# Layer 1's conv, short-conv and gate projections as 512- plus 256-column products, four more modulation vectors by selector products, conv taps through ScalarE

## The chip, the cores and the metric

The kernel runs on one core of a Trainium2 chip. The metric is the device time of one launch in microseconds (us). Where the document speaks of TensorE, VectorE, ScalarE and GpSimd, the profile has PE (with PEld for the loading of weights), DVE, ACT and POOL; SP is the engine that issues most DMAs. 
## The reference

A two-layer trunk on 256 tokens of width 2048. In each layer a vector `c` gives six modulation vectors of 2048 (shift, scale and gate for the mixers, the same for the FFN); the normalised input is scaled and shifted by them, projected to 4288 columns, and these are split among four mixers.

```python
mod = (silu(c) @ w_mod[l] + b_mod[l]).reshape(bn, 6, d)      # 2048 x 12288
h = layer_norm(x) * (1.0 + scale_m) + shift_m
uv, q_c, kv_c, k_r, sb, sc, sh, ag = split(h @ w_in[l])      # 2048 x 4288
y_a = gmlp_mixer(uv)                                         # U, V below
y_b = mla_mixer(q_c, kv_c, k_r)                              # B: attention
y_c = sb * causal_dwconv(sc * sh, sconv_w, 3 taps)           # E * conv3(C)
y_d = silu(layer_norm(causal_dwconv(a * sigmoid(g), 31 taps)))   # D: ag = (a, g)
x = layer_norm(ALPHA * x + (1.0 + gate_m) * (concat(y_a, y_b, y_c, y_d) @ w_out[l]))
h = layer_norm(x) * (1.0 + scale_f) + shift_f
x = layer_norm(ALPHA * x + (1.0 + gate_f) * conv_ffn(h))     # up 2 x 5632, down 5632
```

## The kernel before

**Numbers.** Weights and activations are float32. To run at the rate of the faster matmul type, a weight tile is split in two parts, `whi` (a cast on ScalarE, line 455) and `wlo = w - whi` (a subtraction on VectorE, line 456), and the activations in the same way. A product is then the sum of three: high by high, high by low, low by high. Where activations are not ready in time the kernel multiplies in full float32 ("exact", tiles `wexact`), which needs no split and more time on TensorE.

**Two ways to write the three products.** `group` (line 478) makes, for each block of 128 channels and each of the 16 blocks of the contraction, three products of 256 columns (the tokens). `group2` (line 534), so far used by the FFN's up projection alone, lays the high and the low activations side by side, so that one product of 512 columns gives both terms with the high weights, and a product of 256 columns adds the low weights to the first half. One 512-channel group then fills four PSUM banks instead of two; the second half of each bank is added to the first when the bank is read (`second`, line 1416: a ScalarE copy of the second half, then a VectorE addition). There are six such banks (`accp`).

**Stages.** Layer 0's mixers go through `by_pieces` and are not touched. Layer 1's mixers (from line 1236 on) run the groups U, D, V, B, C, E in this order through `run` and `stream`: load and split one unit of 1 MB, issue the products of the unit before, then do a piece of the modulation stream (`pump`) and some pieces of background work. What a group's accumulators are for is done in `mix_u`, `mix_d`, `mix_v`, `mix_b`, `mix_c`, `mix_e`, at the start of the next group. D covers 1024 columns (a and g), C 1024 (`sc` and `sh`), E 512 (`sb`).

**Background.** The 31-tap convolution of D is a list of small pieces, of which `STEPS` says how many are done per unit. In layer 1 a piece is one tap of one channel block: a multiply-add on VectorE of 128 x 256 (`tap`, line 888); there are 124 of them. In layer 0 a piece is one tap of all four blocks: four ScalarE multiplications into a product tile (line 909, two such tiles in turn) and one VectorE addition of 128 x 1024 (line 910).

**Modulation vectors.** The matrix-vector product runs on VectorE: for each of 16 rows of blocks a multiply-add into an accumulator `macc` of 128 x 2048 (line 250). The sum over the 128 partitions is left to TensorE. `mod_cols` (line 198) multiplies each 128 x 128 block of the accumulator with a column of ones: one column out per product. `mod_rows` (line 220) splits the accumulator in high and low parts like a weight tile (`halves`, taking buffers of the same pool `splitp`, four each), multiplies them by selector columns that put the sum of each 512-column quarter in its own row of a 4 x 512 result, copies this, turns it with four small transposes and adds the bias. Which of the two is used is chosen in `settle`:

```python
elif (l, m) in ((1, SHIFT_F), (1, SCALE_F)):
    mod_rows(l, m, acc)
else:
    mod_cols(l, m, k0, acc[:, k0 * P : k1 * P])
```

So layer 1's FFN vectors go by rows; layer 0's FFN vectors (of which blocks 0 to 11 are summed in the output projection and 12 to 15 later) and layer 1's mixer vectors go by columns. These are needed by `to_hT` at the end of a layer half; its first instruction (`xn`) waits until the vectors are there.

**What sets the order.** The program text gives each instruction a rank. A planner goes through the program with its own estimates of durations and writes for each engine a fixed order: what is ready with the best rank goes next, so work of a later rank can be put ahead where the engine would stand. Tiles come from pools with a fixed number of buffers (11 `slot`, 10 `act`, 4 `tmp`, 4 `whi`, 4 `wlo`, 4 raw); an instruction that needs a new tile waits until one is free.

Of the kernel before, what the change touches and what calls it, by code (L numbers as in the profile page):

```python
# [13 lines left out]
P = 128  # L14
# [40 lines left out]
def encoder_kernel(ctx: ExitStack, tc: tile.TileContext, A: dict, consts: bass.AP, out: bass.AP):  # L55
# [155 lines left out]
            MOD[(l, m, k0 + j)] = cols[:, j : j + 1]  # L211
            MOD_BY[(l, m, k0 + j)] = done.ins.name

    def halves(acc, c0):
        hi = splitp.tile([P, 1024], F32R, tag="whi", name="mhi")
        lo = splitp.tile([P, 1024], F32R, tag="wlo", name="mlo")
        split((hi, lo), acc[:, c0 : c0 + 1024])
        return [(hi[:, i * 512 : (i + 1) * 512], lo[:, i * 512 : (i + 1) * 512]) for i in range(2)]

    def mod_rows(l, m, acc):  # L220

        ps = ms_tile("ps_row")
        for j, pair in enumerate(halves(acc, 0) + halves(acc, 1024)):
            for n, part in enumerate(pair):
                mm(ps[0:4, :], onesR[:, P + 4 * j : P + 4 * j + 4], part, j + n == 0, j + n == 4)
        row = tmp_tile("mrow")
        act.copy(row[0:4, :], ps[0:4, :])
        ps = ms_tile("ps_mod")
        for i in range(4):
            pe.transpose(ps[:, 4 * i : 4 * i + 4], row[0:4, i * P : (i + 1) * P], ident[0:4, 0:4])  # L230
        cols = keep.tile([P, KT], F32, name=f"mod_{l}_{m}")
        done = dve.scalar_tensor_tensor(
            out=cols.rearrange("p (i j) -> p i j", i=4),
            in0=ps[:, 0:KT].rearrange("p (i j) -> p i j", i=4),
            scalar=0.0 if m == SHIFT_F else 1.0,
            in1=bcol[l][:, m * KT : (m + 1) * KT].rearrange("p (j i) -> p i j", i=4),
            op0=ALU.add,
            op1=ALU.add,
        )
        for k in range(KT):  # L240
# [232 lines left out]
    def split(dst, src):  # L473
        hi, lo = dst[:2]
        act.copy(hi, src)  # L475
        dve.tensor_tensor(out=lo, in0=src, in1=hi.bitcast(F32), op=ALU.subtract)  # L476
# [384 lines left out]
    def mixers(l, w_in, Y, hF=None, between=None):  # L861
# [7 lines left out]
        CLB = lambda j: pm[:, 149 + j : 150 + j]  # L869


        def mix_d(cps, _):
            glu = slot("gluD").rearrange("p (j s) -> p j s", j=4)
            for b in range(2):
                sg = tmp_tile("sg")
                act.activation(out=sg, in_=cps[2 + b], func=AF.Sigmoid)
                dve.tensor_tensor(
                    out=glu[:, 2 * b : 2 * b + 2, :],
                    in0=cps[b].rearrange("p (j s) -> p j s", j=2),
                    in1=sg.rearrange("p (j s) -> p j s", j=2),  # L880
                    op=ALU.mult,
                )
            yd = slot("convD").rearrange("p (j s) -> p j s", j=4)
            def tap(j, k):
                if k == 30:
                    ident_act(yd[:, j, :], glu[:, j, :], CW(30, j), CB(j))
                else:
                    dve.scalar_tensor_tensor(
                        out=yd[:, j, 30 - k :],
                        in0=glu[:, j, : S - 30 + k],  # L890
                        scalar=CW(k, j),
                        in1=yd[:, j, 30 - k :],
                        op0=ALU.mult,
                        op1=ALU.add,
                    )

            prods = []

            def taps(k):
                n = S - 30 + k  # L900
                if k == 30:
                    for j in range(4):
                        tap(j, k)
                    return
                if len(prods) < 2:
                    prods.append(act_tile("prodD").rearrange("p (j s) -> p j s", j=4))
# [2 lines left out]
                    act.activation(out=pr[:, j, :n], in_=glu[:, j, :n], func=AF.Copy, scale=CW(k, j))  # L909
                dve.tensor_tensor(out=yd[:, :, 30 - k :], in0=yd[:, :, 30 - k :], in1=pr[:, :, :n], op=ALU.add)  # L910

            if l == 0:
                for k in range(30, -1, -1):
                    background.append(lambda k=k: taps(k))
            else:
                for j in range(4):
                    for k in range(30, -1, -1):
                        background.append(lambda j=j, k=k: tap(j, k))
            background.append(lambda: norm_d(yd))

        def norm_d(yd):
            Y["d"] = slot("yd").rearrange("p (j s) -> p j s", j=4)
# [273 lines left out]
                act.copy(Y["b"][:, 2 * b : 2 * b + 2, :], ps.rearrange("p (j s) -> p j s", j=2))  # L1196


        def mix_c(cps, _):
            ch = slot("chC").rearrange("p (j s) -> p j s", j=4)  # L1200
            for b in range(2):
                sc = tmp_tile("sc")
                act.copy(sc, cps[b])
                dve.tensor_tensor(
# [15 lines left out]
                        op1=ALU.add,  # L1220
                    )

        def mix_e(cps, _):
# [139 lines left out]
    def ffn_up(l, G):  # L1363
# [48 lines left out]

        for c0 in range(0, D_FF, 512):
            gi, j0 = c0 // 512, c0 // P

            def second(cps):

                out = []
                for b in range(2):
                    t = tmp_tile("second").rearrange("p (j s) -> p j s", j=2)  # L1420
                    for i in range(2):
                        act.copy(t[:, i, :], cps[2 * b + i][:, S:])
                        out.append(t[:, i, :])
                return out

            def gated(cps, j0=j0):
                G.append(slot("g").rearrange("p (j s) -> p j s", j=4))
# [191 lines left out]
```

## Time and profile before

| | |
|---|---|
| runs | 2282.78 us median of 3 (2282.72 to 2288.62) |
| profiled execution | 2281.42 us, of which the span of the trace is 2279.7 us |
| granted TensorE clock, mean | 0.991 |
| busy share of PE / DVE / ACT | 98% / 78% / 48% |
| layer 1's mixers after the D group | 1270 to 1435 us of the span |

The views that the prediction quotes: the page (busy shares, the chain of work that ended last); that chain in order of time; the busy time of each engine in chosen stretches, with the clock that TensorE was granted; the instructions of one tile, with count, shortest, median and longest duration in ns; the waits; and the timeline of one engine (start, length, what, and in brackets how long the engine had stood and for whom). A busy TensorE in these views is not TensorE at its peak: a product counts as busy while it waits for its turn in the pipeline, so the spacing of products says more than their durations.

### The profile page before, as it was taken

The numbers are of one execution on the slowest core, as the hardware profiler recorded it, in microseconds if no ns is written. First come the engines' busy times: TensorE is split into PE (matmuls) and PEld (weight loads), VectorE is DVE, ScalarE is ACT, GpSimd is POOL, SyncE is SP. The second block draws the span as 40 slices with busy tenths as digits, with TensorE's granted clock in tenths as the row PEclk, the third lists the DMA queues.
The fourth block names the chain that finished last, engine by engine and source line by source line (L and its number), as shares of the span: only waits on it lengthen the run. The fifth ranks groups of instructions, "written<-read, shape, count | busy, mean of one in ns | idle before, by whom it ended". The sixth has DMA issues, their size and how long they took to land.

```text
span 2279.7 us, 31503 instructions
## 1 busy us (share of the span) xinstructions
PE 2238.7 (98%) x12387; PEld 1934.8 (85%) x12387; DVE 1773.3 (78%) x2183; ACT 1098.2 (48%) x1644; POOL 35.1 (2%) x65
## 2 busy tenths in 40 slices
PE   7999999999999999999999999999999999999998
PEld 5788886798888888888789999889888888888886
DVE  5778988888888888988977899787676565565776
ACT  3356641354455444544454434545544454454553
POOL 0011000000000000000000000000000000000000
PEclk9999999999999999999999999999999999999999
DMA  9999699778888888898777677775666555555554
GB/s 349 385 373 359 256 328 349 249 278 314 311 307 315 314 312 327 303 346 302 273 236 254 201 242 250 271 273 177 240 240 215 192 185 197 191 185 194 187 191 148
DMA packets 228717, 605.21 MB, mean 265 GB/s; under 512 B 14660, under 2 KB 27188, under 8 KB 210900
## 3 DMA queue, kind: packets, MB, share of 16 engines
q1 hardware_dynamic: 227784, 602.30, 74.3%
q8 instruction: 97, 1.59, 0.3%
q0 software_dynamic: 784, 0.90, 0.1%
q14 instruction: 52, 0.43, 0.0%
HBM read 601.05 MB, written 2.10 MB: 265 GB/s over the span
## 4 chain that ended last, share of the span: by engine, by line
PE 88%; DVE 7%; DMA 2%; ACT 2%; issue 1%; POOL 0%; SPq 0%; DVEq 0%; ACTq 0%; POOLq 0%
PE g_c L83 22%; PE v_c L83 22%; PE d L83 20%; PE o L83 7%; PE D_c L83 3%; PE C_c L83 3%; PE B_c L83 2%; PE U_c L83 1%; PE E L83 1%; PE E_c L83 1%; DVE wlo L456 1%; PE ps_mod L83 1%; PE V L83 1%; DVE qacc L250 1%; DVE macc L250 1%
## 5 line engine op out<-in xcount | busy, mean ns | idle before, releaser
L455 ACT CAST whi<-wraw 128x1024 fp32r<-128x1024 f32 (+1 forms) x632 | 643.4, 1043 | 753.1 <-PE g_c L83 217.0
L456 DVE TENSOR_TENSOR wlo<-wraw,whi 128x1024 fp32r<-128x1024 f32 (+1 forms) x632 | 750.5, 1214 | 294.3 <-ACT whi L455 273.2
L83 PE MATMUL d<-whi,a 128*128 128x512 f32 x1344 | 390.3, 391 | 0.9 <-ACT whi L455 0.9
L250 DVE SCALAR_TENSOR_TENSOR macc<-wmod,cact,macc 128x2048 f32<-128x2048 f32 (+2 forms) x174 | 353.9, 2034 | 41.5 <-DMA wmod<-in_w_mod_dram 40.8
L83 PE MATMUL v_c<-hT,whi 128*128 128x512 f32 (+1 forms) x1456 | 343.1, 383 | 0.0
L83 PE MATMUL g_c<-hT,whi 128*128 128x512 f32 (+1 forms) x1344 | 313.5, 380 | 0.0
L83 PEld LDWEIGHTS v_c<-hT,whi 128*128 128x128 f32 x1456 | 264.6, 189 | 48.5
L83 PEld LDWEIGHTS d<-whi,a 128*128 128x128 f32 x1344 | 253.4, 189 | 54.5 <-ACT whi L455 2.2
L83 PEld LDWEIGHTS g_c<-hT,whi 128*128 128x128 f32 x1344 | 243.4, 189 | 43.5 <-DVE second L1436 0.4
L83 PE MATMUL d<-wlo,a 128*128 128x512 f32 x672 | 234.8, 392 | 1.6 <-DVE wlo L456 1.6
L83 PE MATMUL v_c<-hT,wlo 128*128 128x256 f32 x1400 | 190.7, 283 | 0.0
L83 PEld LDWEIGHTS v_c<-hT,wlo 128*128 128x128 f32 x1400 | 183.1, 191 | 6.6
L83 PE MATMUL g_c<-hT,wlo 128*128 128x256 f32 x1280 | 175.8, 283 | 0.0
L83 PEld LDWEIGHTS g_c<-hT,wlo 128*128 128x128 f32 x1280 | 168.2, 191 | 5.9
L83 PEld LDWEIGHTS d<-wlo,a 128*128 128x128 f32 x672 | 126.7, 189 | 30.1 <-DVE wlo L456 3.6
L475 ACT CAST a<-g 128x512 fp32r<-128x512 f32 x132 | 80.8, 619 | 91.1 <-PE d L83 89.4
L83 PE MATMUL o<-whi,a 128*128 128x512 f32 x384 | 111.3, 395 | 0.2 <-ACT whi L455 0.2
L476 DVE TENSOR_TENSOR a<-g,a 128x512 fp32r<-128x512 f32 x132 | 87.7, 684 | 9.2 <-ACT a L475 9.2
L250 DVE SCALAR_TENSOR_TENSOR qacc<-wmod,cact,qacc 128x1024 f32<-128x1024 f32 (+1 forms) x75 | 80.3, 1071 | 12.2 <-DMA wmod<-in_w_mod_dram 9.9
L83 PEld LDWEIGHTS o<-whi,a 128*128 128x128 f32 x384 | 72.7, 190 | 16.4 <-issue 0.7
L83 PE MATMUL D_c<-hT,whi 128*128 128x256 f32 x432 | 83.0, 292 | 2.4 <-ACT hT L475 1.6
L83 PEld LDWEIGHTS D_c<-hT,whi 128*128 128x128 f32 x432 | 69.5, 197 | 4.8 <-ACT hT L475 1.7
(370 smaller groups left out, 2619.1 us busy)
## 6 DMA issues: line engine op xcount, KB each, us to landing
wraw<-in_ffn_w_up_dram SPq DMA_DIRECT2D x168, 1024.0 KB, 5.0
wmod<-in_w_mod_dram SPq DMA_DIRECT2D x134, 1024.0 KB, 6.8
wraw<-in_ffn_w_down_dram SPq DMA_DIRECT2D x88, 1024.0 KB, 5.1
wraw<-in_w_in_dram SPq DMA_DIRECT2D x33, 1024.0 KB, 6.1
wmod<-in_w_mod_dram SPq DMA_DIRECT2D x64, 512.0 KB, 9.4
wraw<-in_w_out_dram SPq DMA_DIRECT2D x26, 1024.0 KB, 6.9
wmod<-in_w_mod_dram SPq DMA_DIRECT2D x32, 768.0 KB, 7.5
wexact<-in_w_in_dram SPq DMA_DIRECT2D x46, 512.0 KB, 7.9
```

The lines of the kernel that those rows point to most:

```text
L83: pe.matmul(o, lhsT, rhs, start=start, stop=stop, skip_group_check=True)
L250: i = dve.scalar_tensor_tensor(out=acc, in0=w, scalar=col, in1=acc, op0=ALU.mult, op1=ALU.add)
L455: act.copy(hi[:, :m], r)
L456: i = dve.tensor_tensor(out=lo[:, :m], in0=r, in1=hi[:, :m].bitcast(F32), op=ALU.subtract)
L475: act.copy(hi, src)
L476: dve.tensor_tensor(out=lo, in0=src, in1=hi.bitcast(F32), op=ALU.subtract)
```

## The change

- Layer 1's D, C and E go through `group2`. D becomes two groups of 512 channels, first the gate half g (`Dg`, folded and put through the sigmoid into a new tile `sgD` by `mix_dg`), then the half a; C becomes `Cs` (folded into a new tile `scC`) and C. `whole` folds four banks into a tile; `mix_d`, `mix_c` and `mix_e` then multiply in place.
- Layer 1's conv taps are done as in layer 0; `STEPS` counts the larger pieces.
- `mod_rows` takes 12 blocks as well as 16, and `settle` uses it for every vector whose first block is 0.
- `second` moves out of `ffn_up` unchanged.

```diff
 STEPS = [
     dict(B=3, C=2, up=2),
-    dict(U=5, V=5, B=4, C=6, E=6, up=2),
+    dict(U=1, V=1, B=1, C=2, E=2, up=2),
 ]
...
-    def halves(acc, c0):
+    def halves(acc, c0, width=1024):
...
-    def mod_rows(l, m, acc):
+    def mod_rows(l, m, acc, n=4):
 
         ps = ms_tile("ps_row")
-        for j, pair in enumerate(halves(acc, 0) + halves(acc, 1024)):
-            for n, part in enumerate(pair):
-                mm(ps[0:4, :], onesR[:, P + 4 * j : P + 4 * j + 4], part, j + n == 0, j + n == 4)
+        parts = [x for c0 in range(0, n * 512, 1024) for x in halves(acc, c0, min(1024, n * 512 - c0))]
+        for j, pair in enumerate(parts):
+            for i, part in enumerate(pair):
+                mm(ps[0:4, :], onesR[:, P + 4 * j : P + 4 * j + 4], part, j + i == 0, j + i == n)
...
-        elif (l, m) in ((1, SHIFT_F), (1, SCALE_F)):
-            mod_rows(l, m, acc)
+        elif k0 == 0:
+            mod_rows(l, m, acc, k1 // 4)
         else:
             mod_cols(l, m, k0, acc[:, k0 * P : k1 * P])
...
+    def second(cps):
+
+        out = []
+        for b in range(2):
+            t = tmp_tile("second").rearrange("p (j s) -> p j s", j=2)
+            for i in range(2):
+                act.copy(t[:, i, :], cps[2 * b + i][:, S:])
+                out.append(t[:, i, :])
+        return out
+
+    def whole(cps, dst):
+
+        for i, t in enumerate(second(cps)):
+            dve.tensor_tensor(out=dst[:, i, :], in0=cps[i][:, :S], in1=t, op=ALU.add)
...
-        def mix_d(cps, _):
+        def mix_d(cps, _=None):
             glu = slot("gluD").rearrange("p (j s) -> p j s", j=4)
-            for b in range(2):
+            if l > 0:
+                whole(cps, glu)
+                dve.tensor_tensor(out=glu, in0=glu, in1=Y["sg"], op=ALU.mult)
+            for b in range(2 if l == 0 else 0):
...
-            if l == 0:
-                for k in range(30, -1, -1):
-                    background.append(lambda k=k: taps(k))
-            else:
-                for j in range(4):
-                    for k in range(30, -1, -1):
-                        background.append(lambda j=j, k=k: tap(j, k))
+            for k in range(30, -1, -1):
+                background.append(lambda k=k: taps(k))
             background.append(lambda: norm_d(yd))
+
+        def mix_dg(cps):
+            Y["sg"] = slot("sgD").rearrange("p (j s) -> p j s", j=4)
+            whole(cps, Y["sg"])
+            act.activation(out=Y["sg"], in_=Y["sg"], func=AF.Sigmoid)
...
+        def mix_cs(cps):
+            Y["sc"] = slot("scC").rearrange("p (j s) -> p j s", j=4)
+            whole(cps, Y["sc"])
+
+        def mix_c(cps, _=None):
             ch = slot("chC").rearrange("p (j s) -> p j s", j=4)
-            for b in range(2):
+            if l > 0:
+                whole(cps, ch)
+                dve.tensor_tensor(out=ch, in0=ch, in1=Y["sc"], op=ALU.mult)
+            for b in range(2 if l == 0 else 0):
...
+        def mix_e(cps, _=None):
             yc = Y["c"]
+            if l > 0:
+                for i, t in enumerate(second(cps)):
+                    dve.tensor_tensor(out=t, in0=cps[i][:, :S], in1=t, op=ALU.add)
+                    dve.tensor_tensor(out=yc[:, i, :], in0=yc[:, i, :], in1=t, op=ALU.mult)
+                return
...
-        run(group(w_in, C_AG, 1024, f"D{l}", mix_d, spare=1))
+        run(group2(w_in, C_AG + 512, f"Dg{l}", mix_dg, spare=2))
+        run(group2(w_in, C_AG, f"D{l}", mix_d))
...
-        run(group(w_in, C_SC, 1024, f"C{l}", mix_c, bg=STEPS[l]["C"]))
+        run(group2(w_in, C_SC, f"Cs{l}", mix_cs, bg=STEPS[l]["C"]))
+        run(group2(w_in, C_SC + 512, f"C{l}", mix_c, bg=STEPS[l]["C"]))
         phase(l, "E")
-        run(group(w_in, C_SB, 512, f"E{l}", mix_e, nk=4, bg=STEPS[l]["E"]))
+        run(group2(w_in, C_SB, f"E{l}", mix_e, bg=STEPS[l]["E"]))
```

More of the change, by code (lines that the diff above doesn't have):

```diff
@@ L212, in mod_cols @@
             MOD_BY[(l, m, k0 + j)] = done.ins.name
-    def halves(acc, c0):
[L215 to L218, printed above, removed]
-    def mod_rows(l, m, acc):
+    def halves(acc, c0, width=1024):
+        hi = splitp.tile([P, 1024], F32R, tag="whi", name="mhi")[:, :width]
+        lo = splitp.tile([P, 1024], F32R, tag="wlo", name="mlo")[:, :width]
+        split((hi, lo), acc[:, c0 : c0 + width])
+        return [(hi[:, i : i + 512], lo[:, i : i + 512]) for i in range(0, width, 512)]
+    def mod_rows(l, m, acc, n=4):
         ps = ms_tile("ps_row")
-        for j, pair in enumerate(halves(acc, 0) + halves(acc, 1024)):
-            for n, part in enumerate(pair):
-                mm(ps[0:4, :], onesR[:, P + 4 * j : P + 4 * j + 4], part, j + n == 0, j + n == 4)
+        parts = [x for c0 in range(0, n * 512, 1024) for x in halves(acc, c0, min(1024, n * 512 - c0))]
+        for j, pair in enumerate(parts):
+            for i, part in enumerate(pair):
+                mm(ps[0:4, :], onesR[:, P + 4 * j : P + 4 * j + 4], part, j + i == 0, j + i == n)
         row = tmp_tile("mrow")
@@ L232, in mod_rows @@
         done = dve.scalar_tensor_tensor(
[L233 to L236, printed above, removed]
+            out=cols.rearrange("p (i j) -> p i j", i=4)[:, :, :n],
+            in0=ps[:, 0:KT].rearrange("p (i j) -> p i j", i=4)[:, :, :n],
+            scalar=0.0 if m in (SHIFT_M, SHIFT_F) else 1.0,
+            in1=bcol[l][:, m * KT : m * KT + 4 * n].rearrange("p (j i) -> p i j", i=4),
             op0=ALU.add,
@@ L239, in mod_rows @@
         )
-        for k in range(KT):
+        for k in range(4 * n):
             at = 4 * (k % 4) + k // 4
@@ L902, in taps @@
                     for j in range(4):
-                        tap(j, k)
+                        ident_act(yd[:, j, :], glu[:, j, :], CW(30, j), CB(j))
                     return
@@ L1221, in mix_c @@
                     )
-        def mix_e(cps, _):
+        def mix_e(cps, _=None):
             yc = Y["c"]
+            if l > 0:
[3 more added lines that the diff above has]
+                return
             for b in range(2):
@@ L1414, in ffn_up @@
             gi, j0 = c0 // 512, c0 // P
[L1416 to L1424, printed above, removed]
             def gated(cps, j0=j0):
```

13 lines of the change are left out of this document (removed).

## The prediction

> **What bounds the kernel now.** I read first the busy shares and the chain of waits on the page, then the same chain in order of time, then the busy time by stretch, and last the rows of the tiles that the change touches.
>
> ```profile
> span 2279.7 us, 31503 instructions
> PE 2238.7 (98%) x12387; PEld 1934.8 (85%) x12387; DVE 1773.3 (78%) x2183; ACT 1098.2 (48%) x1644; POOL 35.1 (2%) x65
> ...
> PE 88%; DVE 7%; DMA 2%; ACT 2%; issue 1%; POOL 0%; SPq 0%; DVEq 0%; ACTq 0%; POOLq 0%
> ```
>
> TensorE holds 88% of the chain that ended last. So time is saved where TensorE has less to do, and lost where another engine makes it wait. The stretch that the change rebuilds is layer 1 after its D group. Its four parts are shown by the first and the third of them and by the sum of the four (1270 to 1435 us); the columns are stretch, length, busy us of PE, PEld, DVE, ACT, POOL, granted clock, DMA share, GB/s:
>
> ```profile
> 1270.00:1305.00 35.00, 33.94 (x196) 29.62 (x194) 34.11 (x63) 18.64 (x25) 2.77 (x5) 1.00 0.50 157
> 1331.00:1406.00 75.00, 74.83 (x532) 69.68 (x533) 71.35 (x127) 29.26 (x48) 1.10 (x1) 1.00 0.70 246
> sum 165.00, PE 163.48 PEld 153.40 DVE 156.38 ACT 74.41 POOL 4.56; mean PE 40.87 PEld 38.35 DVE 39.10 ACT 18.60 POOL 1.14
> ```
>
> VectorE is as full there (156.4 of 165 us) as TensorE, and ScalarE is half empty (74.4). Yet VectorE seldom stops TensorE: the longest such wait listed there is this one.
>
> ```profile
> PE B_c L83 <- DVE wlo L456: 1.2, 1, 1.2
> ```
>
> So what is taken from VectorE there can bring about 1 us, not the tens that are taken off it.
>
> **The products.** From the chain in order of time (start, length, what, records):
>
> ```profile
> 1224.12 44.52 PE D_c L83 x371
> 1406.06 17.28 PE E_c L83 x144
> 1559.17 22.26 PE v_c L83 x128
> ```
>
> D and E go by three 256-column products: 17.28 / 144 = 0.120 us each, and 44.52 / 371 the same. A 512-channel group has 16 x 4 x 3 = 192 of them, 23.0 us. The FFN's group2, which D, C and E of layer 1 now use, does the same work in 64 + 64 products in 22.26 us. Saved: 0.77 us a group; D counts two groups, C two, E one, so **-3.9 us**.
>
> [...]
>
> **The modulation sums.** Four vectors move from mod_cols to mod_rows: SHIFT_F and SCALE_F of layer 0 (12 blocks) and SHIFT_M and SCALE_M of layer 1 (16). The late quarter (478 us) and the opening pieces keep mod_cols. The chain shows the old sums inside stages that TensorE bounds, and the new kind inside an FFN group of layer 0:
>
> ```profile
> 341.27 3.03 PE ps_mod L83 x28
> 393.89 2.57 PE ps_mod L83 x24
> 752.58 22.26 PE g_c L83 x128
> 777.02 1.62 PE v_c L83 x7
> 799.62 22.27 PE g_c L83 x128
> 1039.22 1.68 PE ps_mod L83 x16
> 1041.93 2.14 PE ps_mod L83 x20
> 1118.96 3.46 PE ps_mod L83 x32
> ```
>
> Old: 3.03 + 2.57 + (1.68 + 2.14) + 3.46 = 12.9 us. New: the v_c group from 774.84 to 799.62 holds one mod_rows of 16 blocks and lasts 24.78 instead of 22.27 us, so 2.5 us, its waits included. With 12 blocks two of its eight 512-column products fall away, each (22.26 - 64 x 0.120) / 64 = 0.23 us: 2.0 us. New sum 2 x 2.5 + 2 x 2.0 = 9.0. Saved: **-3.9 us**.
>
> **The clock behind the sums.** In these stretches the last-but-two column is the granted clock:
>
> ```profile
> 335.00:338.00 3.00, 3.00 (x15) 2.49 (x14) 2.77 (x2) 0.00 (x0) 0.00 (x0) 1.00 0.84 246
> 344.30:347.70 3.40, 3.40 (x10) 2.65 (x10) 3.36 (x2) 0.07 (x1) 0.00 (x0) 0.54 0.97 355
> 397.00:400.00 3.00, 3.00 (x9) 1.33 (x8) 1.05 (x4) 0.00 (x0) 0.00 (x0) 1.00 1.05 388
> 774.00:800.00 26.00, 26.00 (x151) 21.85 (x150) 24.28 (x29) 15.99 (x27) 0.00 (x0) 1.00 0.79 284
> 1043.00:1047.00 4.00, 4.00 (x18) 3.39 (x18) 1.98 (x2) 2.06 (x3) 0.00 (x0) 0.66 0.83 314
> 1122.40:1126.00 3.60, 3.60 (x11) 2.83 (x11) 2.30 (x2) 2.15 (x3) 0.00 (x0) 0.56 0.88 284
> ```
>
> Behind three of the four old sums the clock falls to about half for some 3.4 us; behind the one at 393.89, the shortest, it stays (row of 397). Around mod_rows at 774 it stays at 1.00. [...] Cost: 3.4 x (1 - 0.54) = 1.6, 4.0 x (1 - 0.66) = 1.4, 3.6 x (1 - 0.56) = 1.6. Removed: **-4.6 us**.
>
> [...]
>
> **Added work on the other engines.** In the tile views (count, then min/median/max ns):
>
> ```profile
> L888 DVE SCALAR_TENSOR_TENSOR convD<-gluD,pm,convD x120: 428/464/481, 1274.2 to 1399.2; 128x255 f32<-128x255 f32 x4, 128x254 f32<-128x254 f32 x4, 128x253 f32<-128x253 f32 x4, 128x252 f32<-128x252 f32 x4
> L909 ACT ACTIVATE prodD<-gluD,pm x120: 467/482/509, 190.4 to 276.2; 128x255 f32<-128x255 f32 x4, 128x253 f32<-128x253 f32 x4, 128x254 f32<-128x254 f32 x4, 128x252 f32<-128x252 f32 x4
> L910 DVE TENSOR_TENSOR convD<-convD,prodD x30: 1072/1156/1207, 193.5 to 280.3; 128x1020 f32<-128x1020 f32 x1, 128x1016 f32<-128x1016 f32 x1, 128x1012 f32<-128x1012 f32 x1, 128x1008 f32<-128x1008 f32 x1
>   DVE convD L910: 17.9, 11
> L1422 ACT COPY second<-v_c x84: 358/376/397, 526.7 to 2027.1; 128x256 f32<-128x256 f32 x84
> L1436 DVE TENSOR_TENSOR second<-v_c,second x84: 415/418/426, 527.1 to 2029.1; 128x256 f32<-128x256 f32 x84
> ```
>
> Taps: VectorE loses 120 x 0.464 = 55.7 and gains 30 x 1.156 = 34.7; ScalarE gains 120 x 0.482 = 57.8. Folding the second halves costs 4 copies and 4 additions a group: over Cs, C and E 12 x 0.376 = 4.5 on ScalarE and 12 x 0.418 = 5.0 on VectorE; the extra products in place are near what the old 512-wide ones cost. VectorE goes to about 156.4 - 55.7 + 34.7 + 5 = 140, ScalarE to 74.4 + 57.8 + 4.5 = 137, of a stretch that becomes about 160 us. Both hide behind TensorE as long as the weight casts, which share ScalarE's queue, stay on time: four split buffers hold two units ahead. In the C group a unit of 5.6 us asks ScalarE for two casts (2.1) and two taps (3.9), already 6.0; the attention block's products, which lie between, make room. From VectorE's relief I take the 1.2 us wait: **-1.0**. For hold-ups of casts behind taps, the lower end is nothing and the upper is layer 0's 17.9 us of ScalarE standing for convD (the fourth row); nearest to the lower end, since ScalarE keeps some 23 us free: **+2.0**.
>
> Banks: Dg to D, Cs to C, C to E and E to the output projection now pass four of six banks on; the lower end is nothing, the upper one folding of a bank pair (2 x 0.376 + 2 x 0.418 = 1.6 us) each, 6.4. The FFN passes them on the same way at 22.26 us a group, so **+0.5**. The two more tiles (sgD, scC) and the two product buffers fit the pools by my count of what is alive; nothing taken.
>
> Where the sums run: mod_rows needs split buffers and 2 x 1.2 us of VectorE per 16 blocks, mod_cols needed neither. For layer 1's two vectors VectorE has gaps of 4.38 and 1.40 us right behind the old sums, and ScalarE's casts wait there for DMA, so that buffers are free:
>
> ```profile
> L476 DVE TENSOR_TENSOR mlo<-macc,mhi x12: 1205/1220/1226, 260.2 to 2147.6; 128x1024 fp32r<-128x1024 f32 x12
> 1045.02 2.36 DVE L456 TENSOR_TENSOR wlo<-wraw,whi 128x1024 fp32r<-128x1024 f32 x2 [4.38 <-ACT whi L455]
> 1123.70 2.36 DVE L456 TENSOR_TENSOR wlo<-wraw,whi 128x1024 fp32r<-128x1024 f32 x2 [1.40 <-ACT whi L455]
> ACT whi L455 <- DMA wraw<-in_ffn_w_down_dram: 11.1, 7, 3.0
> ```
>
> Nothing to 2.4 us; taken 0. For layer 0's SCALE_F the accumulator ends late, while the next weights take the buffers:
>
> ```profile
> 390.33 1.81 DVE L250 SCALAR_TENSOR_TENSOR macc<-wmod,cact,macc 128x1536 f32<-128x1536 f32 x1
> 385.68 5.18 SPq L433 DMA_DIRECT2D wexact<-in_w_out_dram  x6
> 390.96 5.34 SPq L433 DMA_DIRECT2D wexact<-in_ffn_w_up_dram  x4
> 413.58 3.60 PE L83 MATMUL o<-wexact,yd 128*128 128x512 f32 x8
> 417.94 1.36 PE L594 MATMUL ps_xT<-cst,xn 128*128 128x128 f32 x8 [0.77 <-ACT xn L86]
> ```
>
> If the FFN's weights (third row) get the free buffers first, the second half of SCALE_F waits for the last products (until about 417) and needs some 3.3 us more, and xn, which waits for every modulation vector, and all FFN products stand behind it. Nothing to 3.3; **+1.0**.
>
> **Sum.** -3.9 - 3.9 - 4.6 - 1.0 + 2.0 + 0.5 + 1.0 = -9.9. Against the profiled execution's 2281.42 us this gives 2271.5; the median of the runs lies 1.4 above that execution, so I forecast **2273** for the median.
>
> **Rivals.** [...] *The vectors come late* at both layer ends: splits wait for buffers that the tail holds. Twice 3.3 instead of +1.0 once is +5.6: 2278.6. For it: xn is the first thing that TensorE waits for there (0.77). Against: the free buffers in layer 0's last stage, just shown. *ScalarE becomes the bound* in layer 1's B, C and E, the case of the other side: each of 30 taps holds the cast behind it as layer 0's eleven did (17.9 / 11 = 1.6 us), 49 us, of which the 23 us that ScalarE has free swallow their part; 26 us would land on TensorE instead of the 2.0 above: 2273 + 24 = 2297. It decides once casts come more than two units late. For it: 6.0 us asked per 5.6 us unit. Against: layer 0's waits came while VectorE was full. [...]
>
> **How the numbers follow.** Forecast as it stands, 2266 to 2276: 0.58. Clock 0.10, late vectors 0.10, ScalarE 0.14 (half of it over the bound below, half a milder 2280), merging or a shifted order of instructions 0.08. 0.3% is 6.8 us, about what a measurement of this kernel tells from no change: under 2275.9 is faster, over 2289.6 slower. Faster: 0.55 of the 0.58 and 0.05 from the mild ends of the others; slower: 0.07; the rest the same. The range runs from the full gain with no new cost (-13.4, 2269.4) less 4 for a lucky clock elsewhere, to the milder ScalarE case with both vectors late, 2286.
>
> **What would show it.** Right: no granted clock near 0.5 behind SHIFT_F, SHIFT_M and SCALE_M; D, C and E groups at 22.3 us; TensorE in 1270 to 1435 shorter by 3 to 4 us; ScalarE there near 137 us. Wrong: waits of TensorE for whi or wlo in layer 1's C, a gap over 1 us before the first transposes of xn, or ScalarE idle for convD before late casts.

## The result, and the profile after

The change makes the kernel slower: 2301.28 us median (2298.63 to 2309.67) against 2283.36 us (2282.72 to 2288.62) for the kernel before, a ratio of 1.0078 with a 95% interval of 1.0059 to 1.0097. The profiled execution took 2304.15 us, with a span of 2302.4 us, 22.7 us over that of before (2279.7). The forecast was 2273, its range ended at 2286: it was wrong, in sign too.

The page of the changed kernel, its span, busy shares and the shares of the chain that ended last:

```profile
span 2302.4 us, 30825 instructions
PE 2234.0 (97%) x11991; PEld 1909.8 (83%) x11991; DVE 1775.1 (77%) x2125; ACT 1156.0 (50%) x1789; POOL 37.7 (2%) x65
...
PE 85%; DVE 7%; DMA 4%; ACT 2%; issue 2%; POOL 0%; SPq 0%; DVEq 0%; ACTq 0%; POOLq 0%
```

TensorE is busy 4.7 us less than before, and the kernel lasts 22.7 us more. So the work went down as planned, and TensorE now waits where it did not wait. The chain in order of time (start, length, what, records) says in its gaps where; here the end of layer 0 and the first two groups of layer 1 that the change rebuilt:

```profile
1198.14 1.96 PE ps_row L83 x8
...
1212.08 1.97 PE ps_xT L610 x8
...
1247.40 22.29 PE Dg_c L83 x128
1269.69 22.27 PE D_c L83 x128
```

The two rebuilt groups last 22.3 us each, as forecast. But twelve microseconds lie between the last sum of a modulation vector (`ps_row`) and the first transposes of the normalised input (`ps_xT`). The timeline of TensorE shows the same at both ends of layer 0's second half, after the output projection `o` and after the down projection `d` (the brackets: idle before it, and for whom):

```profile
409.67 3.60 PE L83 MATMUL o<-wexact,yd 128*128 128x512 f32 x8
...
417.88 0.41 PE L231 MATMUL ps_mod<-cst,mrow 4*128 4x4 f32 x4 [0.66 <-ACT mrow L228]
428.79 1.97 PE L610 MATMUL ps_xT<-cst,xn 128*128 128x128 f32 x8 [10.50 <-ACT xn L86]
...
1194.78 0.39 PE L83 MATMUL d<-whi,a 128*128 128x512 f32 x1
...
1200.75 0.41 PE L231 MATMUL ps_mod<-cst,mrow 4*128 4x4 f32 x4 [0.66 <-ACT mrow L228]
1212.08 1.97 PE L610 MATMUL ps_xT<-cst,xn 128*128 128x128 f32 x8 [10.92 <-ACT xn L86]
```

Before, the wait for `xn` after `o` was 0.77 us (a row of the prediction). Now it is 10.50 and 10.92, and ahead of each the sums run in the open, after the stage's last product, for about 6 us. In each wait the clock falls to 0.50, and it stays there until 4.4 and 6.2 us after the products have begun again; the windows of TensorE (stretch, length, busy us of PE, PEld, DVE, ACT, POOL, granted clock, DMA share, GB/s):

```profile
419.50:433.20 13.70, 4.41 (x20) 4.22 (x21) 12.54 (x32) 8.07 (x19) 2.54 (x3) 0.50 0.36 130
1204.60:1218.30 13.70, 6.22 (x29) 6.04 (x30) 12.20 (x30) 8.77 (x20) 1.47 (x2) 0.50 0.17 63
```

**What is late, and why.** `xn` is made by ScalarE at the end of the normalisation of the first token tile, a chain of VectorE instructions that begins with `yg`. First the kernel before (timeline of VectorE), then the kernel after:

```profile
406.91 0.69 DVE L701 TENSOR_TENSOR yg<-o,gate 128x512 f32<-128x512 f32 x1 [8.79 <-PE o L83]
...
416.82 0.16 DVE L762 SCALAR_TENSOR_TENSOR rs_o0r<-m_o,rs_o0r 128x1 f32<-128x1 f32 x1 [0.67 <-POOL rs_o0r L114]
```

```profile
396.80 1.22 DVE L477 TENSOR_TENSOR mlo<-macc,mhi 128x1024 fp32r<-128x1024 f32 x1
409.92 0.69 DVE L477 TENSOR_TENSOR mlo<-macc,mhi 128x512 fp32r<-128x512 f32 x1 [11.90 <-issue]
413.36 1.99 DVE L477 TENSOR_TENSOR mlo<-macc,mhi 128x1024 fp32r<-128x1024 f32 x2 [2.74 <-PE o L83]
...
415.85 0.68 DVE L717 TENSOR_TENSOR yg<-o,gate 128x512 f32<-128x512 f32 x1
...
427.67 0.16 DVE L778 SCALAR_TENSOR_TENSOR rs_o0r<-m_o,rs_o0r 128x1 f32<-128x1 f32 x1 [0.67 <-POOL rs_o0r L114]
```

Before, `yg` started when the first token tile's products were done, 9.7 us ahead of the start of the last product (416.58, by the start times). The normalisation ran for some 10 us under the second token tile's products and cost TensorE nothing but its last microsecond. After, the four subtractions `mlo` (the last two in one row) that split the accumulators of layer 0's two FFN vectors stand ahead of `yg` in VectorE's fixed order, and the second and third of them wait 11.90 and 2.74 us. `yg` starts at 415.85, after the start of the last product (412.67), and the same normalisation now runs with TensorE standing by. The subtractions follow the casts `mhi` on ScalarE. Its timeline, at both ends, and VectorE's at the second:

```profile
408.15 0.62 ACT L476 CAST mhi<-macc 128x512 fp32r<-128x512 f32 x1 [16.12 <-PE o L83]
411.58 1.04 ACT L476 CAST mhi<-macc 128x1024 fp32r<-128x1024 f32 x1 [2.82 <-PE o L83]
...
1192.49 1.05 ACT L476 CAST mhi<-macc 128x1024 fp32r<-128x1024 f32 x1 [11.35 <-PE d L83]
```

```profile
1193.57 5.08 DVE L477 TENSOR_TENSOR mlo<-macc,mhi 128x1024 fp32r<-128x1024 f32 x4 [10.99 <-ACT mhi L476]
...
1198.65 0.68 DVE L717 TENSOR_TENSOR yg<-d,gate 128x512 f32<-128x512 f32 x1
```

A cast of an accumulator reads nothing that `o` or `d` makes. The profile infers that one of their products released it, and I read this as the wait for a buffer which that product was still using: the split buffers are held by the last chunk's weights until the last products. So the order is: products of the last chunk, split of the vectors, and only then the normalisation that before ran under these products.

### The profile page after: what moved, and what is told of

It reads as the page before. It is cut to its first block, busy times and chain, and to the rows that moved or that the text cites. A ratio compares the mean times of both kernels' runs of the same rounds, so it can differ in the third digit from the quotient of the medians.

```text
span 2302.4 us, 30825 instructions
## 1 busy us (share of the span) xinstructions
PE 2234.0 (97%) x11991; PEld 1909.8 (83%) x11991; DVE 1775.1 (77%) x2125; ACT 1156.0 (50%) x1789; POOL 37.7 (2%) x65
## 4 chain that ended last, share of the span: by engine, by line
PE 85%; DVE 7%; DMA 4%; ACT 2%; issue 2%; POOL 0%; SPq 0%; DVEq 0%; ACTq 0%; POOLq 0%
PE g_c L83 22%; PE v_c L83 21%; PE d L83 17%; PE o L83 6%; PE C_c L83 3%; PE D_c L83 2%; PE B_c L83 2%; DVE wlo L457 2%; PE U_c L83 1%; DVE qacc L251 1%; DVE macc L251 1%; DMA wmod<-in_w_mod_dram 1%; PE E L83 1%; DMA wraw<-in_ffn_w_down_dram 1%; PE Cs_c L83 1%
## 5 line engine op out<-in xcount | busy, mean ns | idle before, releaser
L915 ACT ACTIVATE prodD<-gluD,pm 128x255 f32<-128x255 f32 (+29 forms) x240 | 98.7, 486 | 29.9 <-DVE convD L916 29.7
L916 DVE TENSOR_TENSOR convD<-convD,prodD 128x1020 f32<-128x1020 f32 (+29 forms) x60 | 69.2, 1154 | 6.0 <-ACT prodD L915 5.4
```

## The experiments

The theory after the two traces: the loss sits wholly in the late vectors, because VectorE waits in the splits (11.90 and 2.74 us after `o`) with the normalisation behind them in its fixed order; the rest of the change is worth about what was forecast. The rivals: ScalarE or the taps hold up layer 1; the sums in rows cost more than they save wherever they stand; the half clock by itself is the loss.

This table gives the stages of the profiled execution of every kernel, worked out from the start times of products in TensorE's timeline (us). "o" and "d" run from the first to the last product of layer 0's projection, "wait" from there to the first transposes of `xn`, "up" from these to `d`, "U" from the transposes to layer 1's D, "D to E" from there to layer 1's output projection, "rest" to the end of the span.

| kernel | o | wait | up | d | wait | U | D to E | rest |
|---|---|---|---|---|---|---|---|---|
| before | 102.9 | 1.4 | 517.7 | 254.8 | 1.0 | 32.4 | 210.7 | 845.1 |
| after | 98.9 | 16.1 | 520.0 | 246.0 | 17.3 | 35.1 | 208.9 | 846.3 |
| e1 vectors early | 105.2 | 1.4 | 517.6 | 249.7 | 1.0 | 32.4 | 209.7 | 845.1 |
| e2 normalisation first | 99.8 | 6.9 | 518.6 | 245.5 | 8.5 | 34.0 | 212.4 | 846.6 |
| e3 no rows | 104.5 | 1.4 | 516.9 | 254.7 | 1.0 | 32.4 | 212.0 | 846.6 |
| e4 rows only | 97.9 | 16.1 | 517.7 | 245.4 | 17.3 | 34.0 | 209.9 | 844.8 |
| f1 products only | 102.9 | 1.4 | 517.1 | 254.9 | 1.0 | 32.4 | 206.9 | 847.5 |
| f2 taps only | 106.8 | 1.4 | 517.8 | 256.4 | 1.0 | 32.4 | 207.5 | 845.1 |
| f3 products, vectors early | 104.9 | 1.4 | 517.9 | 249.7 | 1.0 | 32.4 | 208.3 | 846.5 |
| f4 rows only, early | 104.4 | 1.4 | 518.8 | 249.7 | 1.0 | 32.4 | 211.1 | 846.5 |
| g1 early at `d` alone | 98.2 | 16.1 | 518.9 | 249.7 | 1.0 | 32.4 | 208.8 | 844.8 |
| g2 products, rows for layer 1 | 106.2 | 1.4 | 517.5 | 249.7 | 1.0 | 32.4 | 206.5 | 846.0 |

From before to after this is -4.0 + 14.8 + 2.2 = +13.0 us at the end of the output projection, -8.8 + 16.3 + 2.6 = +10.2 at the end of the down projection, -1.8 in layer 1's D to E and +1.3 in the rest (differences of unrounded times): 22.7. The shorter "o" and "d" of the kernel after are for the greater part no gain: the sums have left the stage and stand behind it, in the wait.

### e1: the vectors one chunk earlier

In the function that ends a chunk of 512 columns, the sums of the vectors are called at the end of the last chunk but one, so that their splits rank ahead of the last chunk's weights:

```diff
                     evacs.pop(0)()
+                    if c0 + 512 == D - 512 and before is not None:
+                        before()
                     return
                 if before is not None:
                     before()
```

> The changed kernel with one call moved: the modulation vectors that the next layer half needs are settled at the end of the output projection's second chunk of columns instead of the third and last, so that their splits rank ahead of the last chunk's weights and of the normalisation. Theory (the splits wait for split buffers that the last chunk holds, and the normalisation of token tile 0 stands behind them on VectorE): the gaps of 10.5 and 10.9 us before the first transposes go back to about 1 us, the clock does not fall there, and the time is 2272 to 2279 us. Rival (ScalarE is what costs, through the conv taps): no better than 2295. Rival (the selector products cost what they cost wherever they stand): the 10 us gaps stay in some form, over 2295.

Measured: 2277.29 us against 2285.70 us, 0.9971 (0.9960 to 0.9982): faster than the kernel before, with all of the change in it. The timeline of TensorE after `o`, and the windows behind both stages:

```profile
419.59 1.36 PE L610 MATMUL ps_xT<-cst,xn 128*128 128x128 f32 x8 [0.77 <-ACT xn L86]
```

```profile
419.00:433.00 14.00, 12.58 (x108) 12.07 (x109) 13.06 (x26) 8.78 (x19) 1.53 (x2) 1.00 0.98 344
1187.50:1201.00 13.50, 13.04 (x114) 12.73 (x115) 11.25 (x21) 10.26 (x23) 1.47 (x2) 1.00 0.98 344
```

The wait is 0.77 us again, the clock is 1.00 in both windows, and "U" is back at 32.4. The same instructions in another order are worth a ratio of 1.0078 / 0.9971 = 1.011. The theory held.

### e2: the normalisation ahead of the sums

Here the sums stay in the last chunk, but the first token tile's normalisation is put ahead of them:

```diff
-                if before is not None:
-                    before()
                 for t in range(2):
                     finish(t, state["ps"], c0)
                     (norm if t == 1 or then is None else second)(t)
+                    if t == 0 and before is not None:
+                        before()
```

> The changed kernel with the vectors settled as late as it does, but behind the normalisation of token tile 0 in the program's order, not ahead of it. Theory (the cost is that the normalisation stands behind the splits on VectorE): the normalisation runs under the second token tile's products again; the vectors still come late, so a gap of 3 to 5 us stays at each of the two layer halves; 2283 to 2291 us. Rival (the lateness of the vectors alone is the cost, as the prediction priced it): the gap is the same 10 to 11 us as in the changed kernel, about 2300.

Measured: 2284.19 us against 2285.70, 0.9993 (0.9981 to 1.0006). The timeline of TensorE after `o`, and the windows behind `o` and behind `d`:

```profile
416.83 0.41 PE L231 MATMUL ps_mod<-cst,mrow 4*128 4x4 f32 x4 [0.72 <-ACT mrow L228]
418.43 1.36 PE L610 MATMUL ps_xT<-cst,xn 128*128 128x128 f32 x8 [1.19 <-ACT xn L86]
```

```profile
418.00:428.00 10.00, 9.52 (x83) 9.21 (x84) 9.26 (x18) 6.18 (x15) 1.48 (x2) 1.00 1.02 365
1191.90:1195.30 3.40, 3.40 (x18) 3.40 (x17) 3.40 (x6) 3.40 (x10) 0.92 (x1) 0.50 0.99 374
```

The splits are as late as in the change and TensorE does the sums in the open as there, but the ten microseconds are gone: the wait for `xn` is 1.19 us (1.18 after `d`). No half clock follows after `o`; after `d` one of 3.4 us does, and "U" takes 34.0 us instead of 32.4. This separates the two costs of a late vector. The sums in the open are what remains, 5.5 and 7.5 us of wait more than before, where I had expected a gap of 3 to 5; the other nine or so at each end were the normalisation held behind the splits on VectorE.

### e3 and e4: without the vectors, and the vectors alone

e3 is the change with the old rule for the vectors; e4 is the kernel before with the vectors' part of the change alone (`halves`, `mod_rows` and the rule in `settle`, as in the diff above).

```diff
-        elif k0 == 0:
+        elif (l, m) in ((1, SHIFT_F), (1, SCALE_F)):
             mod_rows(l, m, acc, k1 // 4)
```

> The changed kernel without its new use of selector products (layer 1's FFN vectors alone by rows, as before). Theory: the loss is all in the vectors, so this is at or a little under the kernel before, 2278 to 2284 us; with the sums by columns back, the clock falls to half for 3.4 us behind some of them. Rival (ScalarE's taps and the folding cost): 2293 or more.

> The kernel before with only the selector products for four more vectors. Theory: the whole loss and more is here, 2300 to 2307 us, with the same two gaps of 10 to 11 us. Rival (ScalarE's taps and the folding cost): near the kernel before, 2275 to 2285.

Measured: e3 2283.55 us against 2285.70, 0.9992 (0.9980 to 1.0004); e4 2298.93 against the same, 1.0077 (1.0053 to 1.0101), a little under the 2300 that I expected at least. The vectors alone lose as much as the whole change (1.0078), and the rest without them loses nothing. The table shows e4 with the same waits, 16.1 and 17.3 us. e3 also shows the clock behind the sums in columns, in the windows behind the four of them:

```profile
342.50:345.90 3.40, 3.40 (x10) 2.61 (x9) 2.79 (x2) 0.93 (x1) 0.00 (x0) 0.50 0.95 337
393.70:397.10 3.40, 3.40 (x8) 1.85 (x8) 2.00 (x5) 0.27 (x1) 0.00 (x0) 0.50 1.05 386
1042.20:1045.60 3.40, 3.40 (x11) 2.82 (x11) 2.05 (x2) 2.06 (x3) 0.00 (x0) 0.50 0.72 278
1120.70:1124.10 3.40, 3.40 (x10) 2.72 (x11) 1.99 (x3) 2.15 (x3) 0.00 (x0) 0.50 0.78 255
```

All four are at half clock for 3.4 us; in the execution of before it was three of four (0.54, 0.66 and 0.56 in the prediction's windows).

### f1 and f2: the products alone, the taps alone

f1 is the kernel before with `group2` for D, C and E of layer 1; the taps stay multiply-adds on VectorE. f2 is the kernel before with the taps alone:

```diff
-    dict(U=5, V=5, B=4, C=6, E=6, up=2),
+    dict(U=1, V=1, B=1, C=2, E=2, up=2),
...
-            if l == 0:
-                for k in range(30, -1, -1):
-                    background.append(lambda k=k: taps(k))
-            else:
-                for j in range(4):
-                    for k in range(30, -1, -1):
-                        background.append(lambda j=j, k=k: tap(j, k))
+            for k in range(30, -1, -1):
+                background.append(lambda k=k: taps(k))
```

> The kernel before with only the product part: layer 1's D, C and E by 512 plus 256 columns, conv taps on VectorE as before, sums by columns as before. Theory (merging saves 0.77 us a group as the rows say, and the taps through ScalarE give part of it back in the attention block): D to E 3 to 4 us shorter than before, no gap of 3 us before ps_pT, 0.998 to 0.999 of the kernel before. Rival (the merge itself is eaten by the folding and the bank hand-over): no shorter, 1.000.

> The kernel before with only the conv taps of layer 1 through ScalarE. Theory (ScalarE's taps delay the attention block's exponentials and TensorE waits for them): 1 to 4 us slower than before, with a gap of about 3 us before one of the ps_pT transposes. Rival (the taps' relief of VectorE pays): 1 us faster, no such gap.

Measured: f1 2280.19 us against 2284.49, 0.9986 (0.9974 to 0.9999), or 3.2 us less (0.2 to 5.9); f2 2283.94, 0.9994 (0.9981 to 1.0007), no difference that can be told. So the time of f1 bears out a gain of the size forecast (3.9 us), and moving the taps brings nothing that shows: in f2 D to E is some 3 us shorter than before, but its output projection, which the taps do not touch, is 3.9 us longer (see g2). Together they do not add up. With products and taps, D to E takes 208.8 to 212.4 us (after, e1, e2, e3, g1), with products alone 206.5 to 208.3 (f1, f3, g2). A part of these differences is the clock, which falls to half for 3.4 us in some executions; the kernel before, then the kernel after:

```profile
1430.00:1433.40 3.40, 3.40 (x16) 3.22 (x15) 2.44 (x6) 1.27 (x2) 0.69 (x1) 0.50 0.88 337
```

```profile
1409.40:1412.80 3.40, 3.40 (x14) 2.88 (x12) 3.40 (x5) 2.28 (x6) 0.00 (x0) 0.50 0.00 0
```

Such a stretch costs an estimated 1.7 us (3.4 at half). In D to E the kernels before, after, e1 and f4 have one each, e2 and e3 two, and the others none. So of the 3.9 us by which this stage is shorter in f1's trace than before, some 1.7 are the clock of that execution. Another part is a wait which only the pair has, seen in the timelines of the kernel after, first TensorE and then VectorE:

```profile
1408.12 0.41 PE L1187 MATMUL ps_pT<-cst,p 128*128 128x128 f32 x2 [2.85 <-DVE p L1178]
```

```profile
1402.80 0.29 DVE L1156 TENSOR_SCALAR ps_sc<-ps_sc 64x128 f32<-64x128 f32 x1
1403.00 1.10 DVE L916 TENSOR_TENSOR convD<-convD,prodD 128x920 f32<-128x920 f32 x1
1404.02 0.68 DVE L1157 TENSOR_REDUCE sm<-ps_sc 128x2 f32<-128x512 f32 x1
1404.62 1.09 DVE L916 TENSOR_TENSOR convD<-convD,prodD 128x916 f32<-128x916 f32 x1
...
1405.84 1.11 DVE L916 TENSOR_TENSOR convD<-convD,prodD 128x912 f32<-128x912 f32 x1
...
1407.62 0.62 DVE L1178 TENSOR_SCALAR p<-p,sm 128x256 f32<-128x256 f32 x2
```

Three of the conv's wide additions (1.1 us each) stand between the steps of attention's softmax, and the transposes of `p` wait 2.85 us (2.86 in e1, e2, e3 and g1). I had expected such a wait in f2 too; it is not there. That the additions cause it is read off the order on VectorE; no run moved them away one by one. The half clock of the kernel after comes with this wait, but not in every execution; g1 across its wait:

```profile
1392.20:1397.00 4.80, 3.73 (x21) 3.15 (x22) 3.82 (x7) 4.10 (x11) 0.00 (x0) 1.00 0.00 0
```

### f3 and f4: the parts that are worth keeping

f3 is f1 with all four vectors by rows and the early call of e1; f4 is e4 with the early call, and nothing else of the change.

> Products and selector products with the vectors settled at the end of the second chunk, conv taps left on VectorE: the version that beats all the others by the theory. 0.994 to 0.9965 of the kernel before, under the version with taps on ScalarE (0.9971) by 1 to 3 us. Rival (taps through ScalarE are worth having): 0.9975 or more.

> The kernel before with only the selector products, settled at the end of the second chunk. Theory: what the vectors bring when they are in time, about the difference between the early version and the one without rows (6 us): 0.997 to 0.998, the output projection's part of it near nothing because that stage waits for DMA, the down projection's part some 5 us; no slow clock behind the sums. As the prediction priced it: 8.5 us, 0.9963. Rival (rows bring nothing even in time): 0.9995 to 1.001.

Measured, against 2284.49 us: f3 2276.94, 0.9965 (0.9952 to 0.9977); f4 2278.06, 0.9971 (0.9957 to 0.9984). f3, which leaves the taps on VectorE, beats the kernel before and the changed one. It cannot be told from e1 or f4 (0.9971 both), so what the products and the taps add beside the vectors is not shown by these three. f4 against e4 is the reordering by itself again, 1.0077 to 0.9971. In f4 the sums by rows stand at 389.4 to 397.2 and at 1120.5 to 1131.3 us, and the granted clock is 1.00 around them, also where it was 0.50 to 0.56 behind sums in columns (e3 and before):

```profile
342.10:404.00 61.90, 59.91 (x204) 35.88 (x205) 48.85 (x51) 12.40 (x14) 0.00 (x0) 1.00 0.94 344
1120.00:1140.00 20.00, 19.32 (x89) 13.53 (x88) 19.07 (x27) 13.64 (x18) 0.00 (x0) 1.00 0.54 177
```

The rows gain in the down projection, 249.7 us instead of 254.7 to 256.4, in each of the kernels that has them early. They gain nothing that can be relied on in the output projection: 104.4 to 105.2, against 102.9 to 106.8 in the kernels with sums in columns. f4's timelines of TensorE and of ScalarE show one reason:

```profile
340.89 1.19 PE L83 MATMUL o<-whi,a 128*128 128x512 f32 x4 [0.64 <-ACT whi L456]
...
348.16 1.19 PE L83 MATMUL o<-whi,a 128*128 128x512 f32 x4 [1.14 <-ACT whi L456]
```

```profile
339.79 2.00 ACT L456 CAST whi<-wraw 128x1024 fp32r<-128x1024 f32 x2 [6.14 <-DMA wraw<-in_w_out_dram]
...
382.76 1.06 ACT L476 CAST mhi<-macc 128x1024 fp32r<-128x1024 f32 x1 [1.89 <-PE o L83]
```

TensorE waits 1.8 us in this stage for casts of weights, and the one at 339.79 had itself waited 6.14 us for the transfer of `w_out`. In the kernel before the first sum in columns ran at 341.27 (a row of the prediction), about where TensorE now waits, and no product of the stage waits for a cast. The splits of the vectors are not the reason: the first of them comes at 382.76, and the kernel after, whose first is at 390.98, has waits of the same kind (1.5 us).

### g1: one layer end at a time

The early call only in the down projection:

```diff
-                    if c0 + 512 == D - 512 and before is not None:
+                    if c0 + 512 == D - 512 and before is not None and nkt == NF:
                         before()
```

> The change with the vectors of the layer's last quarter summed one chunk earlier, as in the first experiment, but only in the down projection of layer 0; the output projection keeps the order of the change. Theory (each layer end loses by itself: VectorE's subtractions for the vectors stand ahead of the first token tile's normalisation, some 9 us of wait, and the clock at half behind it): the gap ahead of the transposes stays 10.7 us after the output projection, with a clock near 0.5 for some 13.7 us behind it, and is about 1 us after the down projection, with no slow clock there. The time is half of the way between the first experiment and the change: some 12 us over the first experiment, 1.002 to 1.005 times the kernel before. Rival (the loss sits at one end, the other wait only shifts what follows): a time within 3 us of the change (1.007 to 1.009) or within 3 us of the first experiment (0.996 to 0.998).

Measured: 2290.79 us against 2285.53, 1.0025 (1.0016 to 1.0034). That lies 0.0054 over e1 and 0.0053 under the change: each end costs about 12 us by itself. The timeline of TensorE and the window after `o`:

```profile
429.17 1.97 PE L610 MATMUL ps_xT<-cst,xn 128*128 128x128 f32 x8 [10.49 <-ACT xn L86]
```

```profile
421.30:435.00 13.70, 5.83 (x27) 5.64 (x28) 12.61 (x31) 8.08 (x19) 2.01 (x3) 0.50 0.24 91
```

The end that was left as in the change has its wait and its half clock; the other has a wait of 1.0 us in the table. The rival, that the two are not independent, falls.

### g2: rows for layer 1's vectors alone

f3 with layer 0's FFN vectors by columns at their old place, and the early call as in g1:

```diff
-        elif k0 == 0:
+        elif l == 1:
             mod_rows(l, m, acc, k1 // 4)
```

> The wider products and the early sums, taps on VectorE as before, and selector products only for layer 1's vectors; layer 0's FFN vectors are summed column by column at their old place. Theory (in the output projection the sums lay partly under the wait for w_out's transfer, so rows bring nothing there): the output projection takes about 103 us as before instead of 104 to 105, the clock falls to half for 3.4 us near 342 us again, the down projection stays at 249 to 250 us; the time is 0 to 3 us under that of the wider products with all four vectors early, 0.995 to 0.9965 times the kernel before. Rival (rows save in both stages alike): 2 to 4 us above that kernel, 0.9975 to 0.9985.

Measured: 2277.35 us against 2285.53, 0.9971 (0.9960 to 0.9982). The output projection took 106.2 us, not the 103 that I expected, and the ratio lies between the two expectations; its interval holds f3's 0.9965. Whether rows or columns are better in the output projection is not settled by the times. But the traces show what sets its length where the sums go by columns. The windows of g2 behind its two sums:

```profile
344.40:351.20 6.80, 6.80 (x22) 5.74 (x22) 6.07 (x5) 2.16 (x3) 0.00 (x0) 0.50 1.00 370
399.10:402.50 3.40, 3.40 (x6) 1.52 (x6) 1.72 (x5) 0.27 (x1) 0.00 (x0) 0.50 1.05 387
```

That is 10.2 us at half clock, as in f2 (341.8 to 348.6 and 396.4 to 399.8). e3 has 6.8 (its first two windows above), before and f1 have 3.4, behind the first sum alone. By the estimate of 1.7 us for each 3.4, the 102.9 us of before and f1 become 104.6 for e3 and 106.3 for f2 and g2; the table has 104.5, 106.8 and 106.2. The code is the same in all five.

## Why the prediction was wrong

**The step that failed** is the last of the costs, "Where the sums run". The forecast took +1.0 us for layer 0's SCALE_F (0 to 3.3) and 0 for layer 1's two vectors (0 to 2.4), and in the rival *the vectors come late* twice 3.3. Measured, each end costs some 12 us (g1). That rival had the wait for buffers right and its price wrong. Two things went wrong in this step.

- I priced the vectors' own lateness, and of layer 0's two only the second half of SCALE_F: a split and a few products that `xn` must wait for. In the trace three of the four halves are late (the casts at 408.15, 411.58 and 414.00). I did not ask what stands behind the waiting split on VectorE. It is the first token tile's normalisation, 10 us long, which cost nothing only because the second token tile's products covered it. e2 shows this part: with the normalisation ahead of the splits the wait falls from 10.5 to 1.2 us after `o` and the ratio goes from 1.0078 to 0.9993, four fifths of the way to e1. In the kernel after the split at 409.92 had waited 11.90 us, and `yg` came only behind the splits, at 415.85.
- For layer 1's vectors I read free buffers from the gaps at 1045 and 1124, the place of the old sums. But the sums did not stay there: the splits ran at 1192 to 1199, when the last products gave the buffers free. That the buffers released them is read from the trace. In e1 both rank and buffers come earlier at once; splits with buffers of their own would tell the two apart, and no run did this.

A second cost was missing with it: the half clock that came with these waits (10.50 and 10.92 us in the kernel after, 10.49 in g1), 13.7 us at 0.50. After the first wait 4.4 us of it fall on products, which at half speed lose an estimated 2.2 us; after the second, "U" takes 34.0 (e4) to 35.1 us (after) instead of 32.4. I had looked for the clock only behind the sums themselves.

**What was right**, by the forecast's own terms, with the vectors put early (e1, f3, f4) so that they can be seen:

- Merged products, -3.9: D's two groups took 22.3 us each, and f1 is 3.2 us (0.2 to 5.9) faster. Right in size, as far as that interval tells. The whole stretch from the D groups to the output projection took 164.1 us in the kernel after (1292.0 to 1456.1), not the 160 forecast, with the wait of 2.85 us and a half clock in it.
- Modulation sums and the clock behind them: the forecast for the down projection comes to -(3.82 + 3.46 - 5.0) - 3.0 = -5.3, and it took 5.1 us less. Right. For the output projection it comes to -(5.6 - 4.0) - 1.6 = -3.2, and no gain was measured. Wrong there: TensorE waits for weights in the time that the sums no longer take (1.8 us in f4), and with sums in columns the cost of the clock varied between kernels with the same code there, from an estimated 1.7 us in before and f1 to some 5 in f2 and g2.
- The clock stays up around sums by rows that stand among products (f4's windows at 1.00): right, and the 0.10 that the prediction gives to "Clock" is not borne out for these. Around sums in the open it fell once in e2 (0.50 from 1191.9 us, for 3.4 us). The lower end of the range takes another 4 us for a lucky clock elsewhere. No run shows that term; the runs showed half clock behind the two sums of the output projection for 3.4, 6.8 or 10.2 us with the same code, an estimated 1.7 to 5 us.
- Taps: VectorE's relief of -1.0 and the casts' +2.0 were estimates on both sides of nothing, and f2 measures nothing. ScalarE, forecast at 137 us in the stretch, was busy 119.7 of its 164.1 us and did not become the bound. A smaller cost came from another place: the conv's additions within the softmax (2.85 us), only beside the merged products.
- Banks, +0.5: TensorE waits 0.49 us in f1 and 0.96 in f3 for the folding of C (`chC`) before E's first products, and 0.47 to 0.96 in e1, e2, e3 and g1 for `scC` before C's. Right in size.

With the vectors early the change measured 2277.29 us (e1) and without the taps 2276.94 (f3): the likeliest case's own range was 2266 to 2276, and the gain measured (0.0029 and 0.0035 of 2285, some 6.6 and 8.0 us) is somewhat under the 9.9 of the sum. So the other terms together came to two thirds to four fifths of what was forecast, and the sign hung on the one that I priced by the wait alone. The rival on the slow side was the wrong one too: it named ScalarE, at 2297, and the loss came from VectorE's order.

What the prediction named as a sign of being wrong, "a gap over 1 us before the first transposes of xn", is what the trace of after shows.

## What to carry to other kernels

When an instruction is moved or added that waits for a buffer, go down its engine's fixed order and price what stands behind it, not the instruction: here a few microseconds of splits held back ten microseconds of normalisation that had been free. Work that hides under the last products of a stage loses its cover all at once if it starts later than those products end, and here a halved clock came with the wait (0.50 over 13.7 us). What the next stage needs first should have a rank, and its buffers, ahead of the current stage's last loads.

## What was not expected of the hardware

- With a wait of 10.5 us TensorE ran at a clock of 0.50 over 13.7 us, of which some 4.4 us lay after the products had begun again (428.79 to 433.20). Shorter gaps came with it in some runs only. The wait of 2.85 us in the softmax comes with 3.4 us at half clock in the kernel after (1409.4), e1 (1380.8) and e3 (1383.6); in e2 and g1 a wait of 2.86 us there leaves the clock at 1.00 (f1 and f2, above). So a gap just under 3 us came with half the clock in three of five traces, and so did sums with gaps of at most 1.18 us after `d` in e2 (1191.9). What sets it off is not shown.
- Behind the four sums of one-column products the clock was 0.50 in e3, and behind three of them 0.54 to 0.66 in the kernel before, though the profile counts TensorE as busy all through (3.03 of 3.03 us in the first sum of before, 3.40 of 3.40 in each of e3's windows). A busy share of 100% did not mean a clock of 1.00 here.
- The same code was at half clock for 3.4 (before, f1), 6.8 (e3) or 10.2 us (f2, g2) behind its two sums in the output projection, and the stage lasted 102.9 to 106.8 us with it. So one trace alone does not carry a term of 3 us there, and the clock of a stretch is to be read before two traces of it are compared.
